# A gated scan whose two token halves run as two interleaved chains on shared split weights, with outputs laid out by token

## The chip, the core and the metric

The kernel runs on one core of a Trainium2 chip. That core has TensorE (PE in the profile; PEld is its weight load), VectorE (DVE), ScalarE (ACT), GpSimd (POOL) and SyncE (SP). Each engine executes its own instructions in the order in which they stand in its queue and waits for others by semaphores. The metric is the time of one launch on the device in microseconds (us).

## What is computed

A two-layer encoder on 1024 tokens of width 1024, in fp32. Layer 0 is windowed attention with a feed-forward block; layer 1 replaces attention by a bidirectional gated linear scan (HGRN2) of 8 heads of 128 keys and 128 values. The change touches only that scan. Cut to what matters:

```python
def step(state, inp):                       # one chunk of tokens, one direction
    qc, kc, vc, gc = inp
    b = jnp.cumsum(gc, axis=2)
    inter = jnp.einsum('bhtk,bhkv->bhtv', qc * jnp.exp(b), state)
    ...
    scores = jnp.einsum('bhtk,bhsk,bhtsk->bhts', qc, kc, decay)
    intra = jnp.einsum('bhts,bhsv->bhtv', scores, vc)
    ...
    return new_state, inter + intra
...
z = h @ w_in                                # q, f forward, f backward, v, gate
logf_f, k_f = forget(z[..., o1:o2], lb_fwd) # f = lb + (1-lb)*sigmoid, k = (1-lb)*(1-sigmoid)
...
o = out_f + out_b
o = o * lax.rsqrt(jnp.mean(o * o, axis=-1, keepdims=True) + LN_EPS) * norm_g
o = o * jax.nn.silu(gate)
return o.reshape(B, S, HGRN_VW) @ w_o
```

## The kernel before, in words

Every large product is made of three fp32r matmuls: operands are split into a high part (a ScalarE cast, line 73) and a low part (a subtraction on VectorE or GpSimd, line 74), and `mm3` (lines 349 to 351) multiplies high by high, high by low and low by high. Tokens come in two halves `h` of 512. Activations stand with features on partitions and tokens along the free axis; a pool `acts` of 49 buffers of 128x512 (function `A`) holds most of them, 32 of which are the split input X of the layer.

In the scan stage (`hgrn`), head `n` and half `h` go through these steps:

- `proj`: three projections `z(i, n, h)` of 24 matmuls each into a PSUM tile `zps`; ScalarE's sigmoid `sg`; VectorE makes the decay F and the key K for both directions from it (lines 1044, 1045), then the query and its two decayed forms Q (lines 1048, 1052). `v_proj` makes the values of two heads at once (`hvps`).
- `levels`: the scores of each block of 128 tokens are built in seven levels of doubling block size. In a level ScalarE copies K to `ks` (line 1074), VectorE multiplies K by the decay `cur` (line 1079), TensorE makes four 128x128 products `lv` (line 1082; two matmul instructions each in the profile), and VectorE multiplies both halves of Q (lines 1087, 1089), makes the decay of the next size `tot` (line 1093) and copies `lv` under a mask into the scores `sc` (line 1095). Q of a level waits for `lv` of that level, `lv` of the next level waits for Q and `ks`. Level 0 and the diagonal use sums over partitions by a matmul with ones (`average`, lines 395, 396).
- `states`: transposes of K (`tr`, `kt`), the products `u` with the values, and the running states S, a sequence of small VectorE operations over the four blocks.
- `out`: the output `op` with values on partitions (line 1162), then the root mean square over partitions by squares, a sum with ones (`ms`), a root on ScalarE, VectorE's reciprocal (line 1170) and a product (line 1172).
- `gate`: the fourth projection and two VectorE operations (lines 1036, 1037) which leave the gated output in `O`, in SBUF until the output projection (`hops`).

`weave(main, side, ratio)` runs two generators, one step of `main` and `ratio` steps of `side` at a time. Here `main` is the projections of the next half and a gate, `side` is `work`: levels, states and out of the present half. So before the change one chain of levels is under way at a time, and every projection weight is loaded and split twice, once per half (GpSimd makes the low part of `w_hz` and `w_hv`). `plan_all` lists the weights in the order in which they are taken. A scheduler then sets the final order on each engine from what is written, and a buffer that is taken again waits for its last reader.

## Time and profile before

| | us |
|---|---|
| median of three runs (2856.09 to 2858.42) | 2856.47 |
| the profiled execution | 2853.95 |
| its span in the trace | 2852.1 |
| attention, layer 0's feed-forward and its gate, up to | 1247 |
| gated scan, 1247 to 1955 | 708 |
| output projection of the scan, 1955 to 2050 | 95 |
| layer 1's feed-forward and gate, 2050 to 2852 | 802 |

TensorE is busy 95% of the span, VectorE 71%, GpSimd 48%, ScalarE 45%; the mean granted clock of TensorE is 0.985. In the rows below, "zps<-xh_n,w_hz" reads: writes tile zps, from tiles xh_n and w_hz; "[0.58 <-PE lv L1082]" is idle time before an instruction and what ended it. A line of a group has its count (x512), busy us, mean ns of one, and after the second bar the idle time before the group's instructions.

### The profile page before, as it was taken

How to read it: one execution, taken by the hardware profiler on the slowest of the kernel's cores; microseconds unless marked ns; L12 is line 12 of the kernel's file. 1: busy time of each engine (PE TensorE's matmuls, PEld its weight loads, DVE VectorE, ACT ScalarE, POOL GpSimd, SP SyncE). 2: the span in 40 equal slices, each digit the busy share in tenths (PEclk: the TensorE clock that was granted, in tenths of full speed). 3: DMA queues.
4: the chain of work that ended last, by engine and by line, in shares of the span. 5: the costliest groups of instructions: out<-in, count | busy, mean ns of one | idle time of the engine just before them, and what ended most of it. 6: DMA issues, size and time to landing. Idle time of an engine off the chain costs nothing.

```text
span 2852.1 us, 37180 instructions
## 1 busy us (share of the span) xinstructions
PE 2699.7 (95%) x12820; PEld 2173.5 (76%) x12820; DVE 2014.7 (71%) x2933; ACT 1283.2 (45%) x2334; POOL 1367.1 (48%) x958
## 2 busy tenths in 40 slices
PE   8999998999999999999998999989989999999999
PEld 6666676788887787787787877878767888878777
DVE  6778887755554658848888888898886555556685
ACT  4555667233333445534444443444462333344463
POOL 4243232656555747653443433331436556556563
PEclk9999999999999999999999999999999999999999
DMA  4111135444445953221111211112355444478243
GB/s 163 49 42 46 43 120 203 164 165 166 148 159 193 363 160 107 89 63 60 56 64 45 74 55 57 63 51 76 103 189 195 156 159 141 154 270 304 81 159 115
DMA packets 194877, 361.40 MB, mean 127 GB/s; under 512 B 22144, under 2 KB 24960, under 8 KB 194688
## 3 DMA queue, kind: packets, MB, share of 16 engines
q1 hardware_dynamic: 150624, 278.78, 29.4%
q10 hardware_dynamic: 44064, 80.24, 7.8%
q8 instruction: 101, 1.65, 0.2%
q14 instruction: 88, 0.72, 0.1%
HBM read 274.52 MB, written 84.41 MB: 126 GB/s over the span
## 4 chain that ended last, share of the span: by engine, by line
PE 36%; DVE 12%; issue 4%; POOL 3%; ACT 2%; DMA 1%; SPq 0%; ACTq 0%; POOLq 0%; DVEq 0%
PE x L349 3%; PE x L351 3%; PE x L350 3%; PE zps L351 2%; PE zps L349 2%; PE zps L350 2%; PE lv L1082 2%; POOL wo L74 2%; PE op L1162 1%; DVE K L1079 1%; PE zy L349 1%; PE zy L351 1%; PE zy L350 1%; DVE Q L1052 1%; PE pgps L350 1%
## 5 line engine op out<-in xcount | busy, mean ns | idle before, releaser
L74 POOL TENSOR_TENSOR w_hz<-r_hz,w_hz 128x512 fp32r<-128x512 f32 x128 | 180.6, 1418 | 332.4 <-ACT w_hz L73 323.0
L74 DVE TENSOR_TENSOR wp<-wraw,wp 128x512 fp32r<-128x512 f32 x200 | 210.7, 1054 | 163.2 <-ACT wp L73 135.8
L74 DVE TENSOR_TENSOR hs<-wraw,hs 128x512 fp32r<-128x512 f32 x154 | 210.9, 1388 | 139.7 <-ACT hs L73 136.4
L74 POOL TENSOR_TENSOR wo<-wraw,wo 128x512 fp32r<-128x512 f32 x154 | 225.7, 1478 | 158.1 <-ACT wo L73 143.5
L73 ACT CAST wp<-wraw 128x512 fp32r<-128x512 f32 x200 | 124.5, 623 | 295.5 <-PE x L351 149.0
L349 PE MATMUL x<-xc,wp 128*128 128x512 f32 x528 | 211.5, 402 | 12.6 <-ACT u L734 9.5
L349 PE MATMUL zps<-xh_n,w_hz 128*128 128x512 f32 x512 | 212.7, 415 | 0.0
L351 PE MATMUL x<-xc,wp 128*128 128x512 f32 x528 | 210.9, 400 | 0.0
L350 PE MATMUL x<-xc,wp 128*128 128x512 f32 x528 | 210.2, 398 | 0.0
L351 PE MATMUL zps<-xh_n,w_hz 128*128 128x512 f32 x512 | 202.4, 395 | 0.0
L350 PE MATMUL zps<-xl_n,w_hz 128*128 128x512 f32 x512 | 201.3, 393 | 0.0
L73 ACT CAST wo<-wraw 128x512 fp32r<-128x512 f32 x154 | 95.4, 620 | 188.7 <-POOL wo L74 114.4
L349 PE MATMUL ox<-hs,wo 128*128 128x512 f32 x352 | 138.4, 397 | 12.6 <-ACT hs L73 12.6
L186 POOL TENSOR_TENSOR wraw<-s,wraw 128x512 f32<-128x512 f32 x34 | 45.0, 1325 | 203.7 <-DVE wp L74 203.7
L351 PE MATMUL ox<-hs,wo 128*128 128x512 f32 x352 | 138.6, 394 | 1.6 <-POOL wo L74 1.6
L350 PE MATMUL ox<-hs,wo 128*128 128x512 f32 x352 | 138.8, 394 | 0.7 <-DVE hs L74 0.7
L349 PEld LDWEIGHTS x<-xc,wp 128*128 128x128 f32 x528 | 100.1, 190 | 40.0 <-ACT u L734 10.3
L1082 PEld LDWEIGHTS lv<-Q,ks 128*128 128x128 f32 x768 | 97.8, 191 | 37.3 <-issue 25.1
L1074 ACT COPY ks<-K 128x512 f32<-128x512 f32 x96 | 60.6, 631 | 145.4 <-DVE K L1079 111.3
L1082 PE MATMUL lv<-Q,ks 128*128 128x128 f32 x768 | 105.4, 279 | 20.4 <-DVE tot L1093 10.3
L73 ACT CAST w_hz<-r_hz 128x512 fp32r<-128x512 f32 x128 | 79.0, 618 | 89.8 <-issue 42.4
L351 PEld LDWEIGHTS x<-xc,wp 128*128 128x128 f32 x528 | 100.0, 189 | 25.3 <-DVE wp L74 0.6
(376 smaller groups left out, 8420.2 us busy)
## 6 DMA issues: line engine op xcount, KB each, us to landing
wraw<-in_wfi_dram SPq DMA_DIRECT2D x196, 256.0 KB, 3.1
wraw<-in_wfo_dram SPq DMA_DIRECT2D x154, 256.0 KB, 4.1
wraw<-h SPq DMA_DIRECT2D x154, 256.0 KB, 4.8
r_hz<-in_whg_dram SPq DMA_DIRECT2D x128, 256.0 KB, 2.8
wraw<-w SPq DMA_DIRECT2D x88, 256.0 KB, 5.3
w<-wraw ACTq DMA_DIRECT2D x66, 256.0 KB, 3.1
h<-th ACTq DMA_DIRECT2D x66, 256.0 KB, 2.1
r_pg<-in_wpg_dram SPq DMA_DIRECT2D x32, 512.0 KB, 3.8
```

The costliest lines, as they stand in the source:

```text
L73: act.copy(hi, src)
L74: (eng or dve).tensor_tensor(lo, src, f32(hi), op=ALU.subtract)
L186: pool.tensor_tensor(a11, tmp, a11, op=ALU.subtract)
L349: pe.matmul(ps, lhsT=w[0], rhs=x[0], start=start, stop=False, skip_group_check=free)
L350: pe.matmul(ps, lhsT=w[0], rhs=x[1], start=False, stop=False, skip_group_check=free)
L351: pe.matmul(ps, lhsT=w[1], rhs=x[0], start=False, stop=stop, skip_group_check=free)
L1052: dve.tensor_tensor(Qq[:, 1 - d], qk[:, 0], Fg[:, d], op=ALU.mult)
L1074: act.copy(view(ks, 0, [[2 * B, g], [B, 2], [1, B]]), kv)
L1079: dve.tensor_tensor(kv, kv, view(cur, off + 1, [[2, g], [row - 1, 2], [0, B]]), op=ALU.mult)
L1082: pe.matmul(lv[:, c], lhsT=ks[:, c * P:(c + 1) * P], rhs=view(Qq, c * P, dims), start=True, stop=True)
L1162: pe.matmul(op[:, cs], lhsT=a, rhs=b, start=i == 0, stop=i == len(ops) - 1)
```

## The change

Both halves of a head now run together. `proj` takes each weight once and multiplies it with both halves; `work(n)` advances the levels of half 0 and half 1 in turn (`both`, which takes one step of each of two generators), then states and out of both. Head 0 alone runs its halves one after the other. F and K are made on ScalarE by activations with scale and bias. The output is computed transposed, with tokens on partitions (`sc` and Q are now the stationary side): the sum of squares comes from ScalarE's accumulating Square in four blocks, the root from a GpSimd power and three small VectorE operations with one refining step, and the scaling from four ScalarE activations. `gated` transposes the output back on TensorE (`otr`), multiplies it by the gate, and stores it to DRAM (heads 0 to 6) until `split_o` reads it back. Gates come two heads later, within the next `proj`. Values, ks and states move from their own tags to the common pool of 49; F, K, qk, tot and Q get more buffers.

```diff
                 for i in (1, 2, 0):
                     z(i, n)
+                    if i == 1 and n > 1:
+                        z(3, n - 2)
 
             ffn(0)
             load(0)
             for n in range(NH):
                 load(n)
-                if n > 1:
-                    z(3, n - 2)
-                if n + 1 < NH:
-                    load(n + 1)
-                if n > 0:
-                    z(3, n - 1)
-                if n + 1 == NH:
-                    z(3, n - 1)
-            z(3, NH - 1)
-            z(3, NH - 1)
+            for n in (NH - 2, NH - 1):
+                z(3, n)
...
+                mh = gp.tile([P, 4], F32, bufs=1, name="mh")
+                dve.memset(mh, -0.5)
+                kept = {(n, h): D_(f"o{n}{h}") for n in range(NH) for h in range(2)}
...
+                    for h in hs:
+                        vt = [A(f"v{n}{h}").rearrange("p (b v) -> p b v", b=4) for n in (2 * pr, 2 * pr + 1)]
+                        V[2 * pr, h], V[2 * pr + 1, h] = vt
...
+                            for i in range(2):
+                                act.copy(vt[i][:, b], o[:, i * P:(i + 1) * P])
...
+                def z(i, n, hs):
+                    w = take_w("z", i, n)
+                    for h in hs:
+                        ps = yield from lin(w, [X[k][h] for k in range(KT)], "zps")
+                        sg = T("t0", "sg")
+                        act.activation(sg, ps, AF.Sigmoid)
+                        yield h, ps, sg
...
+                def gate(n, late=None):
+                    for r in z(3, n, (0, 1)):
+                        if r:
+                            h, ps, sg = r
+                            gz = A(f"gz{n}{h}") if late is not None else sg
+                            dve.scalar_tensor_tensor(gz, ps, ng[:, 0:1], sg, ALU.mult, ALU.mult)
+                            if late is not None:
+                                late[h] = gz
+                            else:
+                                gated(n, h, gz)
                         yield
...
-                    ps, sg = yield from z(3, n, h)
-                    dve.tensor_tensor(sg, sg, ps, op=ALU.mult)
-                    dve.scalar_tensor_tensor(O[n][h], O[n][h], ng[:, 0:1], sg, ALU.mult, ALU.mult)
-                    Fg, Kk = G("F", f"F{n}{h}", 2), G("K", f"K{n}{h}", 2)
+                def gated(n, h, gz):
+                    tr = aux("otr")
+                    for c in range(4):
+                        pe.transpose(tr[:, c * P:(c + 1) * P], O[n][h][:, c * P:(c + 1) * P], idn)
+                    o = A(f"og{n}{h}")
+                    dve.tensor_tensor(o, gz, tr, op=ALU.mult)
+                    if n < NH - 1:
+                        act.dma_start(kept[n, h], o)
+                    O[n][h] = o
...
+                def proj(n, hs):
+                    for h in hs:
+                        st[n, h] = dict(F=G("F", f"F{n}{h}", 3), K=G("K", f"K{n}{h}", 4))
                     for d in range(2):
-                        _, sg = yield from z(1 + d, n, h)
-                        dve.tensor_scalar(Fg[:, d], sg, om[:, d, n:n + 1], lb[:, d, n:n + 1], ALU.mult, ALU.add)
-                        dve.tensor_scalar(Kk[:, d], sg, 1.0, lbm[:, d, n:n + 1], ALU.subtract, ALU.mult)
-                    ps, sg = yield from z(0, n, h)
-                    qk = G("qk", f"qk{n}{h}", 1)
-                    dve.tensor_tensor(qk[:, 0], sg, ps, op=ALU.mult)
-                    pool.tensor_tensor(qk[:, 1], Kk[:, 0], Kk[:, 1], op=ALU.add)
-                    Qq = G("Q", f"Q{n}{h}", 3)
-                    for d in range(2):
-                        dve.tensor_tensor(Qq[:, 1 - d], qk[:, 0], Fg[:, d], op=ALU.mult)
-                    st[n, h] = dict(F=Fg, K=Kk, qk=qk, Q=Qq)
+                        for r in z(1 + d, n, hs):
+                            if r:
+                                t, sg = st[n, r[0]], r[2]
+                                act.activation(t["F"][:, d], sg, AF.Identity, bias=lb[:, d, n:n + 1], scale=om[:, d, n:n + 1])
+                                act.activation(t["K"][:, d], sg, AF.Identity, bias=om[:, d, n:n + 1], scale=lbm[:, d, n:n + 1])
+                            yield
+                        if d == 0 and n > 1:
+                            yield from gate(n - 2)
+                    for r in z(0, n, hs):
+                        if r:
+                            h, ps, sg = r
+                            t = st[n, h]
+                            qk = t["qk"] = G("qk", f"qk{n}{h}", 2)
+                            dve.tensor_tensor(qk[:, 0], sg, ps, op=ALU.mult)
+                            pool.tensor_tensor(qk[:, 1], t["K"][:, 0], t["K"][:, 1], op=ALU.add)
+                            Qq = t["Q"] = G("Q", f"Q{n}{h}", 4)
+                            for d in range(2):
+                                dve.tensor_tensor(Qq[:, 1 - d], qk[:, 0], t["F"][:, d], op=ALU.mult)
+                        yield
...
-                    tot = G("tot", f"tot{n}{h}", 1)
+                    tot = G("tot", f"tot{n}{h}", 2)
...
-                        ks = G("ks", "ks", 2, (HALF,))
+                        ks = A("ks")
...
-                    Ss = t["S"] = G("S", f"S{n}{h}", 2, (2, 4, P))
+                    Ss = t["S"] = [A(f"S{n}{h}{d}").rearrange("p (c v) -> p c v", c=4) for d in range(2)]
...
-                        ops = [(vt[:, c, vs], t["sc"][:, c])]
-                        if prev is not None:
-                            ops.append((prev, t["Q"][:, 1, cs]))
+                        ops = [(t["sc"][:, c], V[n, h][:, c])]
+                        if c or h:
+                            ops.append((t["Q"][:, 1, cs], t["S"][0][:, c] if c else st[n, 0]["Snext"]))
                         if not (h == 1 and c == 3):
-                            ops.append((t["S"][:, 1, c], t["Q"][:, 0, cs]))
+                            ops.append((t["Q"][:, 0, cs], t["S"][1][:, c]))
...
+                    ms, r = (gp.tile([P, 4], F32, tag=x, bufs=2, name=x) for x in ("ms", "r"))
                     sq = T("t0", "osq")
-                    act.activation(sq, op, AF.Square)
-                    ms = aux("ms")
-                    average(ms, onev, sq)
-                    rs = T("t1", "ors")
-                    act.activation(rs, ms, AF.Sqrt, bias=eps[:, 0:1], scale=1.0 / P)
-                    dve.reciprocal(rs, rs)
+                    for c in range(4):
+                        act.activation(sq[:, c * P:(c + 1) * P], op[:, c * P:(c + 1) * P], AF.Square, accum_out=ms[:, c:c + 1])
+                    dve.tensor_scalar(ms, ms, 1.0 / P, EPS, ALU.mult, ALU.add)
+                    pool.tensor_tensor(r, ms, mh, op=ALU.pow)
+                    dve.tensor_tensor(ms, ms, r, op=ALU.mult)
+                    dve.scalar_tensor_tensor(ms, ms, -0.5, r, ALU.mult, ALU.mult)
+                    dve.scalar_tensor_tensor(ms, ms, 1.5, r, ALU.add, ALU.mult)
+                    yield
                     O[n][h] = A(f"o{n}{h}")
...
-                    dve.tensor_tensor(O[n][h], rs, op, op=ALU.mult)
+                    for c in range(4):
+                        act.activation(O[n][h][:, c * P:(c + 1) * P], op[:, c * P:(c + 1) * P], AF.Identity,
+                                       scale=ms[:, c:c + 1])
...
+                def work(n):
+                    if n == 0:
+                        yield from levels(0, 0)
+                        while "Q" not in st.get((0, 1), ()):
+                            yield
+                        yield from levels(0, 1)
+                    else:
+                        yield from both(levels(n, 0), levels(n, 1))
+                    yield from states(n, 0)
+                    yield from states(n, 1)
+                    yield from both(out(n, 0), out(n, 1))
+
+                gzs = [None, None]
+                weave(load(0, (0,)), pend, 0.75)
                 for n in range(NH):
-                    def main0():
-                        yield from load(n, 1)
-                        if n > 1:
-                            yield from gate(n - 2, 0)
-
-                    def main1():
-                        if n + 1 < NH:
-                            yield from load(n + 1, 0)
-                        if n > 0:
-                            yield from gate(n - 1, 1)
-                        if n + 1 == NH:
-                            yield from gate(n - 1, 0)
-
-                    weave(main0(), work(n, 0), 0.75 if n % 2 else 0.5)
-                    weave(main1(), work(n, 1), 0.5 if n % 2 else 0.75)
+                    if n + 1 < NH:
+                        main = load(n + 1, (0, 1))
+                        if n == 0:
+                            main = chain(load(0, (1,)), main)
+                        count = (40 if n else 53) + (16 if n % 2 else 0)
+                        weave(main, work(n), (20 if n else 27) / count)
                 oh = [[], []]
...
-                    split(hi, lo, O[n][h])
+                    o = O[n][h]
+                    if n < NH - 1:
+                        o = A(f"or{n}{h}")
+                        sync.dma_start(o, kept[n, h])
+                    split(hi, lo, o)
...
-                weave(chain(gate(NH - 1, 0), gate(NH - 1, 1)), chain(out(NH - 1, 0), splits(0, 0, NH - 1), out(NH - 1, 1)), 2)
+                weave(chain(gate(NH - 2), gate(NH - 1, gzs), splits(0, 0, NH - 1)), work(NH - 1), 0.7)
+                for h in range(2):
+                    gated(NH - 1, h, gzs[h])
```

VectorE, the levels of head 4. Before, one chain: level 2 and the start of level 3 of half 0 (names end in head and half: K40 is K of head 4, half 0).

```order
L1079 TENSOR_TENSOR K40_13907<-K40_13907,tot40_14301 128x64x2x4
L1087 TENSOR_TENSOR Q40_14110<-Q40_14110,tot40_14301 128x128x2
L1089 TENSOR_TENSOR Q40_14110<-Q40_14110,tot40_14301 128x128x2
L1095 COPY_PREDICATED sc40_14291<-hm_10950,lv2_14343 128x512
L1093 TENSOR_TENSOR tot40_14301<-tot40_14301 128x2x64
L1079 TENSOR_TENSOR K40_13907<-K40_13907,tot40_14301 128x32x2x8
L1093 TENSOR_TENSOR tot40_14301<-tot40_14301 128x2x32
L1087 TENSOR_TENSOR Q40_14110<-Q40_14110,tot40_14301 128x64x4
```

Now, one round over both chains (K40, then K41):

```order
L1106 TENSOR_TENSOR K40_13938<-K40_13938,tot40_14448 128x64x2x4
L1114 TENSOR_TENSOR Q40_14341<-Q40_14341,tot40_14448 128x64x4
L1116 TENSOR_TENSOR Q40_14341<-Q40_14341,tot40_14448 128x64x4
L1120 TENSOR_TENSOR tot40_14448<-tot40_14448 128x2x64
L1122 COPY_PREDICATED sc40_14438<-hm_10950,lv3_14537 128x512
L1106 TENSOR_TENSOR K41_13940<-K41_13940,tot41_14474 128x64x2x4
L1114 TENSOR_TENSOR Q41_14408<-Q41_14408,tot41_14474 128x64x4
L1116 TENSOR_TENSOR Q41_14408<-Q41_14408,tot41_14474 128x64x4
L1120 TENSOR_TENSOR tot41_14474<-tot41_14474 128x2x64
L1122 COPY_PREDICATED sc41_14464<-hm_10950,lv3_14549 128x512
```

One chain's block of five operations has become two blocks, half 0's and half 1's, with nothing else between them in this head.

VectorE, from the end of a head's outputs to the next head's first level. Before, the two outputs of head 3 inside the first levels of head 4:

```order
L74 TENSOR_TENSOR avl_14150<-osq_14146,avh_14149 128x512
L1170 RECIPROCAL ors_14155<-ors_14155 128x512
L1036 TENSOR_TENSOR sg_14172<-sg_14172,zps_14133 128x512
L1172 TENSOR_TENSOR o31_14158<-ors_14155,op_14093 128x512
L1037 SCALAR_TENSOR_TENSOR o21_13389<-o21_13389,ng_10957,sg_14172 128x512
L74 TENSOR_TENSOR avl_14255<-osq_14251,avh_14254 128x512
L74 TENSOR_TENSOR avl_14295<-qk40_14107,avh_14294 128x512
L1170 RECIPROCAL ors_14260<-ors_14260 128x512
L74 TENSOR_TENSOR avl_14308<-ks_14303,avh_14307 128x512
L1172 TENSOR_TENSOR o30_14263<-ors_14260,op_14213 128x512
```

Now, the outputs of head 3 in front of the first level of head 4:

```order
L1079 TENSOR_TENSOR Q40_14341<-qk40_14338,F40_13937 128x512 x2
L1187 TENSOR_SCALAR ms_14344<-ms_14344 128x4
L1187 TENSOR_SCALAR ms_14356<-ms_14356 128x4
L1189 TENSOR_TENSOR ms_14344<-ms_14344,r_14345 128x4
L1189 TENSOR_TENSOR ms_14356<-ms_14356,r_14357 128x4
L1190 SCALAR_TENSOR_TENSOR ms_14344<-ms_14344,r_14345 128x4
L1190 SCALAR_TENSOR_TENSOR ms_14356<-ms_14356,r_14357 128x4
L1191 SCALAR_TENSOR_TENSOR ms_14344<-ms_14344,r_14345 128x4
L1191 SCALAR_TENSOR_TENSOR ms_14356<-ms_14356,r_14357 128x4
L1104 TENSOR_TENSOR ks_14450<-Q40_14341,K40_13938 128x256 x2
L1114 TENSOR_TENSOR Q40_14341<-Q40_14341,F40_13937 128x256
```

The two reciprocals, the low parts of the squares and the products with the root are gone; eight operations on 128x4 stand in their place, ahead of ks and Q of the next head, and `r` in them comes from GpSimd.

TensorE between two level groups of head 4. Before, from lv3 to lv4 of half 0:

```order
L350 MATMUL zps_14367<-xl_n41_11098,w_hz_12_4_14183 128x512
L351 MATMUL zps_14367<-xh_n41_11097,w_hz_12_4_14183 128x512
L349 MATMUL zps_14367<-xh_n51_11114,w_hz_12_4_14183 128x512
L350 MATMUL zps_14367<-xl_n51_11115,w_hz_12_4_14183 128x512
L351 MATMUL zps_14367<-xh_n51_11114,w_hz_12_4_14183 128x512
L349 MATMUL zps_14367<-xh_n61_11143,w_hz_12_4_14183 128x512
L350 MATMUL zps_14367<-xl_n61_11144,w_hz_12_4_14183 128x512
L351 MATMUL zps_14367<-xh_n61_11143,w_hz_12_4_14183 128x512
L349 MATMUL zps_14367<-xh_n71_11153,w_hz_12_4_14183 128x512
L350 MATMUL zps_14367<-xl_n71_11154,w_hz_12_4_14183 128x512
L351 MATMUL zps_14367<-xh_n71_11153,w_hz_12_4_14183 128x512
L1082 MATMUL lv4_14404<-Q40_14110,ks_14405 128x128 x4
```

Now, from lv4 of half 0 to lv4 of half 1:

```order
L343 MATMUL zps_14530<-xh_n61_11166,w_hz_13_4_14284 128x512
L1109 MATMUL lv4_14573<-Q40_14341,ks_14574 128x128 x4
L344 MATMUL zps_14530<-xl_n61_11167,w_hz_13_4_14284 128x512
L345 MATMUL zps_14530<-xh_n61_11166,w_hz_13_4_14284 128x512
L343 MATMUL zps_14530<-xh_n71_11176,w_hz_13_4_14284 128x512
L344 MATMUL zps_14530<-xl_n71_11177,w_hz_13_4_14284 128x512
L345 MATMUL zps_14530<-xh_n71_11176,w_hz_13_4_14284 128x512
L1109 MATMUL lv4_14585<-Q41_14408,ks_14586 128x128 x4
```

Twelve projection matmuls stood between two level groups; now five stand between the groups of the two halves.

## Rows read from the trace of the kernel before

**Rows 1.** Gated-scan stage: its length, busy time and instructions per engine, granted clock, DMA.

```profile
1247.00:1955.00 708.00, 651.93 (x3809) 557.84 (x3808) 602.12 (x936) 302.00 (x510) 262.94 (x185) 0.99 0.18 60
```

**Rows 2.** Costliest TensorE groups of 1247 to 1965: count, busy us, mean ns, idle before.

```profile
L349 PE MATMUL zps<-xh_n,w_hz 128*128 128x512 f32 x512 | 212.7, 415 | 0.0
L1019 PE MATMUL hvps<-w_hv,xh_n 128*128 128x256 f32 x225 | 64.7, 288 | 0.0
L1082 PE MATMUL lv<-Q,ks 128*128 128x128 f32 x768 | 105.4, 279 | 20.4 <-DVE tot L1093 10.3 <-DVE Q L1089 9.9
L1162 PE MATMUL op<-Q,S 128*128 128x128 f32 x208 | 38.0, 300 | 13.6 <-DVE S L1139 13.6
L1115 PE MATMUL u<-v,kt 128*128 128x128 f32 x256 | 37.1, 291 | 13.4 <-ACT kt L1111 13.4
```

**Rows 3.** TensorE's timeline: start, duration (a row of several: together), instruction.

```profile
1641.33 0.39 PE L351 MATMUL zps<-xh_n,w_hz 128*128 128x512 f32 x1
1641.56 0.60 PE L1109 MATMUL tr<-idn,K 128*128 128x128 f32 x4
1641.91 0.47 PE L349 MATMUL zps<-xh_n,w_hz 128*128 128x512 f32 x1
...
1658.90 1.12 PE L1082 MATMUL lv<-Q,ks 128*128 128x128 f32 x8
1659.77 0.49 PE L349 MATMUL zps<-xh_n,w_hz 128*128 128x512 f32 x1
...
1735.13 0.28 PE L1019 MATMUL hvps<-w_hv,xh_n 128*128 128x256 f32 x1
1735.25 0.28 PE L1020 MATMUL hvps<-w_hv,xl_n 128*128 128x256 f32 x1
```

**Rows 4.** Who TensorE waited for in 1247 to 1965: total us, times, longest.

```profile
PE op L1162 <- DVE S L1139: 13.6, 7, 2.7
PE u L1115 <- ACT kt L1111: 13.4, 6, 2.7
PE lv L1082 <- DVE tot L1093: 10.3, 5, 2.5
PE lv L1082 <- DVE Q L1089: 9.9, 13, 1.4
```

**Rows 5.** VectorE groups of 1247 to 1955, each shape apart: count, busy, mean.

```profile
L1095 DVE COPY_PREDICATED sc<-hm,lv 128x512 f32<-128x512 uint8 x112 | 81.6, 728 | 6.3 <-ACT sc L1062 5.0 <-PE lv L396 0.9
L1079 DVE TENSOR_TENSOR K<-K,tot 128x512 f32<-128x512 f32 x96 | 74.2, 773 | 2.8 <-ACT ks L1074 1.8
L1087 DVE TENSOR_TENSOR Q<-Q,tot 128x256 f32<-128x256 f32 x96 | 73.3, 763 | 15.2 <-PE lv L1082 14.1
L1089 DVE TENSOR_TENSOR Q<-Q,tot 128x256 f32<-128x256 f32 x96 | 62.8, 654 | 0.0
L1170 DVE RECIPROCAL ors<-ors 128x512 f32<-128x512 f32 x14 | 46.9, 3351 | 11.6 <-ACT ors L1169 11.6
L1044 DVE TENSOR_SCALAR F<-sg,om,lb 128x512 f32<-128x512 f32 x32 | 22.3, 697 | 20.2 <-ACT sg L1031 20.0
L1093 DVE TENSOR_TENSOR tot<-tot 128x128 f32<-128x128 f32 x16 | 7.3, 454 | 0.2
```

**Rows 6.** Timeline: a VectorE product started inside a GpSimd subtraction, and two alone.

```profile
1598.43 0.41 DVE L1089 TENSOR_TENSOR Q<-Q,F 128x256 f32<-128x256 f32 x1
1598.76 0.68 DVE L1079 TENSOR_TENSOR K<-K,tot 128x512 f32<-128x512 f32 x1
...
1639.74 1.47 POOL L74 TENSOR_TENSOR w_hz<-r_hz,w_hz 128x512 fp32r<-128x512 f32 x1
1639.99 1.51 DVE L1089 TENSOR_TENSOR Q<-Q,tot 128x256 f32<-128x256 f32 x1
```

**Rows 7.** GpSimd's largest group of 1247 to 1955.

```profile
L74 POOL TENSOR_TENSOR w_hz<-r_hz,w_hz 128x512 fp32r<-128x512 f32 x127 | 178.9, 1416 | 332.4 <-ACT w_hz L73 323.0 <-PE lv L1082 6.6 <-issue 2.0
```

**Rows 8.** ScalarE, whole span: an activation with scale and bias per partition.

```profile
L459 ACT ACTIVATE y<-y,lnt 128x512 f32<-128x512 f32 x48 | 38.0, 813 | 15.2 <-DVE y L458 15.0
```

92 lines of the change are left out of this document (37 added, 55 removed).

## Prediction

> **What bounds the kernel now.** I read the table of stages first, then the costliest groups inside the gated-scan stage, then the timeline of that stage for the pace of single instructions, then who waited for whom. The diff touches only the gated scan, which is the stretch from 1247 to 1955 us; everything before and after it issues the same work. There TensorE shows 651.93 of 708 us busy and VectorE 602.12, while ScalarE has 302 and GpSimd 263 [rows 1]. So TensorE bounds the stage, and VectorE is close behind it at 85%.
>
> A busy TensorE is not one at its pace, so I price its work by start-to-start distance. A 128x512 matmul starts 0.23 us after the one before, a 128x256 one 0.12, a group of eight level matmuls occupies 0.87 until the next projection matmul, four transposes 0.35 [rows 3]. Counts [rows 2]: 3 x 512 projections x 0.23 = 353 us; 3 x 225 value projections x 0.12 = 81; 768 / 8 level groups x 0.87 = 84; 256 state matmuls at 0.87 / 8 = 28; 352 output matmuls (11 products in each of 16 halves, two instructions each; 208 of them are the row's form) at 0.11 = 38; 32 groups of transposes (two per head and half, `states`) x 0.35 = 11; 96 averaging matmuls (lv0, lv1 and ms, two each, in 16 halves) x 0.23 = 22. That is 617 us, so some 92 of the 708 are stalls, refills behind them and slow-clock stretches (granted clock 0.99). This 92 is all that the change can win.
>
> TensorE's named waits are for VectorE or for something that VectorE delayed: `op` for S 13.6 us, `u` for kt 13.4, `lv` for tot 10.3 and for Q 9.9 [rows 4]. The reader should see VectorE running late there, with a reciprocal of 3.35 us per half in its queue [rows 5].
>
> **The change part by part.** TensorE's work is unchanged in sum. Each projection matmul still loads its own weights, so sharing the split weights between halves removes none. The 32 `ms` matmuls go (32 x 0.23 = -7.4 us) and 64 transposes of outputs come (16 x 0.35 = +5.6) [rows 3]: zero within 2 us. The four transposes in rows 3 last 0.60 us together and hold the next projection back by 0.35, one alone being far longer than its share. The Trainium skill (TensorE: Matmul & The Clock Gate, Part 4: PE-mode transpose) gives about 275 ns for a transpose inside a kernel, a rule against this change: 64 of them would be an estimated 17.6 us and the sum 12 us later; the spacing in this trace speaks for 0.09 us each.
>
> VectorE loses, per half: the reciprocal 3.35 us, two F and two K operations (F 0.70 each with its waits, K near it), the product with the root, and the low part of the square: 16 x 3.35 = 54 us and, by F's row taken for both, 64 x 0.70 = 45 us at most are the bulk [rows 5]. It gains four operations on 128x4 per half, far smaller than any row of its group.
>
> GpSimd splits each z weight tile once instead of twice: 64 x 1.416 = 91 us of 263 go, and half of the v weight splits with them [rows 7, 1]. This matters for VectorE: a 128x256 product takes 0.41 us alone and 1.51 us when it starts inside a GpSimd subtraction [rows 6], and the mean of that form in the stage is 0.763 and 0.654 [rows 5].
>
> ScalarE loses half of the casts and all root activations with their table loads; it takes over F and K (64 activations with pointer scale and bias, at most 0.813 us each [rows 8], 52 us) and 128 small activations on 128x128, each below 0.813. At 302 of 708 us [rows 1] it can take that beside TensorE; without that cover each would delay a level's ks copy.
>
> **The price: rounds that VectorE bounds.** Two chains now go through the seven levels side by side, so in a round VectorE does two blocks K, Q, Q, tot, sc. By the mean rows a block is 0.773 + 0.763 + 0.654 + 0.454 + 0.728 = 3.37 us [rows 5]; an instruction ends about 0.07 after the next one starts (0.41 long, the next 0.33 behind [rows 6]), so 3.02, or 6.0 a round. Without GpSimd beside it K is 0.68 and Q 0.41 [rows 6]; with tot at 0.3 (estimate, its row less the same interference) a block is 2.53 - 0.35 = 2.2 and a round 4.4. With GpSimd's splits halved I take the middle, 5.2; the ends are 4.4 and 6.0.
>
> In heads 2, 4, 6 the other half of TensorE's queue is z projections, and the new order puts 52 of them between lv2 and lv7 of head 4, beside ten level groups: (52 x 0.23 + 10 x 0.87 + 0.35) / 5 rounds = 4.2 us a round. So TensorE waits 1.0 us in each of 6 rounds, 18 us in three heads. In heads 1, 3, 5 a round has 24 to 30 value matmuls and two level groups, 4.6 to 5.3 us: 0.3 a round, 5 us. Head 7 has only the two last gates beside it: 6 us in its rounds. After its last level the chain transposes, kt, u, S, op, squares, power, O, otr, gate product, split runs with little else in the queue, and hops needs its end; some 10 us (estimate: about 13 us of dependent steps, against 15 hops matmuls, 3.4 us). Before, this last chain was shorter on its queue: one half was already out.
>
> At the end of each other head the three small VectorE operations wait for the GpSimd power. That operation stands in no row; between nothing and 1.42 us, a full tile's subtraction [rows 7], which is the nearest row, and I take the upper end, two per head. Behind it in VectorE's queue stand ks and Q of the next head's first level, and lv0 and lv1 on TensorE wait for these. The new order has 36 to 48 matmuls between op and lv0 (9.7 to 10.9 us) as cover; squares of both halves, a split in front, two powers, small products, ks, its cast and its low part are about as long. I take 1.5 us in seven heads, 10 us. Head 0 keeps its single chains (8 us, its share of 92 being about 11), and slow-clock stretches some 7 (clock 0.99).
>
> Output stores and reloads (28 x 256 KB) replace 80 weight loads of that size, at a DMA share of 0.18 [rows 1]; their issues sit on ScalarE's and SyncE's queues behind products that are done well before; I take nothing, and a reload that is late would show as ScalarE waiting before the first hops.
>
> Sum of stalls after: 18 + 5 + 6 + 10 + 10 + 8 + 7 = 64 against 92, so -28 us. The profiled execution took 2853.95 us; 2826. The median of the runs, 2856.47, stands 2.5 above it, so the forecast for runs is 2828.
>
> **Rivals.**
> Slower: VectorE's rounds stay at 6.04 us because the remaining GpSimd work falls into the rounds. Then 24 rounds (heads 2, 4, 6, 7) lose 1.84 and 18 lose 1.14: 65 us instead of the 29 counted above, +36: 2864. It beats the old time from a round of about 5.9 us up. For it: VectorE was 85% busy with one chain; against it: some 110 us of GpSimd work are gone.
> Much faster: rounds at 4.4 us lose 0.2 in 24 rounds, 5 us, the ends of heads are covered and the tail costs 5: stalls 25, -67: 2790. For it: all of TensorE's named waits are on late VectorE work; against it: even heads have only 4.2 us of TensorE work in a round.
> No change: the power waits behind a 1.42 us split on GpSimd twice per head, and VectorE, blocked, starts the next head 3.5 us late in seven heads: +25 on the forecast, 2853. For it: nothing in VectorE's queue may pass the waiting operation; against it: the 10 us of cover.
>
> **How the numbers follow.** Forecast 0.48, much faster 0.24, no change 0.12, slower 0.16. What this measurement tells from no change is about 0.2%, 5.7 us. Faster: 0.48 + 0.24 and a little of the third, 0.74; same 0.10; slower 0.16. The range for eight in ten is 2795 to 2862; the forecast's own range, from the two ends of a round (4.4 and 6.0, half-way each), is 2812 to 2845.
>
> **What would show it.** In the new profile the gated-scan stage should be near 680 us, VectorE busy about 450 there, GpSimd about 150. The Q product should fall from 0.76 to near 0.6 us mean. Rounds of heads 2, 4, 6 should last about 5.2 us, with TensorE's `lv` waiting for Q; in heads 1, 3, 5 it should hardly wait. `u` waiting for kt and `op` for S should shrink from 13 us each to a few, save in head 7. If VectorE is over 540 busy, or rounds exceed 5.9 us, the forecast is wrong towards slower; if `lv0` waits come to over 20 us, the power chain is the reason.

## The result and the profile after

The changed kernel takes 2837.3 us (2829.9 to 2839.3) against 2857.4 (2856.1 to 2860.5) before, both run on the same chip: ratio 0.9927, 95% interval 0.9914 to 0.9939. It is faster by 20 us, 0.7%. The forecast was 2828, the range 2795 to 2862. Direction and range held; the working behind them held in part only.

The profiled execution lasted 2838.45 us (span 2836.7). The first row is the gated-scan stage of the changed kernel in the columns of [rows 1]. Then come two of its stretches: the start of a head and the level rounds behind it. The number after the five engines is the granted clock.

```profile
1247.00:1930.00 683.00, 646.86 (x3845) 562.92 (x3843) 431.89 (x876) 286.52 (x642) 183.96 (x137) 0.98 0.13 41
...
1639.00:1648.00 9.00, 6.91 (x19) 4.77 (x20) 8.47 (x12) 3.63 (x7) 3.27 (x2) 0.62 0.09 29
1649.00:1675.00 26.00, 25.91 (x159) 22.33 (x159) 25.70 (x61) 11.78 (x20) 2.92 (x2) 1.00 0.06 21
```

VectorE's busy time fell from 602 to 432 us and GpSimd's from 263 to 184. In the rounds TensorE is busy without a gap at full clock. In the start of the same head it stands idle for a quarter of the time, and the mean granted clock of those 9 us is 0.62. Who TensorE waited for in the stage (total, times, longest) answers to [rows 4]:

```profile
PE lv L389 <- ACT avh L73: 14.1, 8, 2.7
PE lv L390 <- DVE avl L74: 12.1, 9, 2.5
PE op L1181 <- DVE S L1166: 2.7, 3, 0.9
PE lv L1109 <- DVE Q L1116: 2.0, 4, 0.7
PE u L1140 <- ACT kt L1136: 1.6, 3, 0.7
```

The four waits of before, 47 us, came down to 8 (6 here and 1.5 for an S of another line). The waits at L389 and L390, the two averages that open a head (lv0 and lv1), grew to 26 us; before, at the same two places, they were 6:

```profile
PE lv L395 <- ACT avh L73: 3.3, 4, 1.0
PE lv L396 <- DVE avl L74: 2.6, 4, 1.0
```

VectorE's, GpSimd's and ScalarE's groups in the changed kernel answer to [rows 5, 7, 8]; L1188 is the power that stood in no row before:

```profile
L1106 DVE TENSOR_TENSOR K<-K,tot 128x512 f32<-128x512 f32 x96 | 69.5, 732 | 1.7 <-ACT ks L1101 1.6
L1079 DVE TENSOR_TENSOR Q<-qk,F 128x512 f32<-128x512 f32 x32 | 44.7, 1434 | 0.3
L1114 DVE TENSOR_TENSOR Q<-Q,tot 128x256 f32<-128x256 f32 x96 | 44.6, 465 | 17.1 <-PE lv L1109 16.7
L1116 DVE TENSOR_TENSOR Q<-Q,tot 128x256 f32<-128x256 f32 x96 | 43.4, 452 | 0.0
```

```profile
L74 POOL TENSOR_TENSOR w_hz<-r_hz,w_hz 128x512 fp32r<-128x512 f32 x69 | 94.4, 1374 | 301.1 <-ACT w_hz L73 292.9 <-DVE S L1160 5.7 <-PE u L1140 2.5
L1188 POOL TENSOR_TENSOR r<-ms,mh 128x4 f32<-128x4 f32 x14 | 14.1, 1016 | 20.3 <-DVE ms L1187 20.3
```

```profile
L1065 ACT ACTIVATE F<-sg,lb,om 128x512 f32<-128x512 f32 x32 | 26.2, 819 | 0.3
```

The two Q products of a level fell from 0.763 and 0.654 us to 0.465 and 0.452, near the 0.41 that one takes alone [rows 6]. The new order of a start is in the timeline (start, duration, instruction):

```profile
1632.96 1.01 POOL L1188 TENSOR_TENSOR r<-ms,mh 128x4 f32<-128x4 f32 x1
1633.02 0.16 DVE L1189 TENSOR_TENSOR ms<-ms,r 128x4 f32<-128x4 f32 x1 [1.06 <-POOL r L1188]
1633.94 1.29 POOL L74 TENSOR_TENSOR w_hz<-r_hz,w_hz 128x512 fp32r<-128x512 f32 x1
1634.01 1.25 DVE L1189 TENSOR_TENSOR ms<-ms,r 128x4 f32<-128x4 f32 x1 [0.82 <-POOL r L1188]
...
1635.57 0.75 DVE L1104 TENSOR_TENSOR ks<-Q,K 128x256 f32<-128x256 f32 x2
1635.62 2.18 ACT L1195 ACTIVATE o<-op,ms 128x128 f32<-128x128 f32 x8 [4.16 <-DVE ms L1191]
1638.11 0.68 ACT L73 CAST avh<-qk 128x512 fp32r<-128x512 f32 x1
1638.84 0.50 PE L389 MATMUL lv<-avh,onev 128*128 128x512 f32 x1 [2.65 <-ACT avh L73]
1639.15 1.59 POOL L1087 TENSOR_TENSOR qk<-qk 128x512 f32<-128x512 f32 x1 [3.91 <-DVE qk L1075]
1639.52 3.44 DVE L1079 TENSOR_TENSOR Q<-qk,F 128x512 f32<-128x512 f32 x2
1642.89 0.68 DVE L74 TENSOR_TENSOR avl<-ks,avh 128x512 fp32r<-128x512 f32 x1
1643.62 0.79 PE L390 MATMUL lv<-avl,onev 128*128 128x512 f32 x1 [1.77 <-DVE avl L74]
```

ScalarE stood 4.16 us before the scalings of O, which wait for the power's chain, and the cast that TensorE needs stood behind them. Later two Q products took 3.44 us beside GpSimd's qk product and a split, and the low part for the next average stood behind these. The 128x4 product that lasts 0.16 us at 1633.02, inside a power, took 1.25 at 1634.01, ending 0.03 us after the subtraction it had started inside.

To say where time went, I took every pair of TensorE instructions that follow each other from the first value projection to the last output projection, and counted by how much their start distance exceeds the usual one of such a pair (its tenth percentile over the kernels compared). The usual distances sum to 706 us before and 706 after, so TensorE's work is unchanged by this count. The excess by part of a head (starts: from a head's first average to its level rounds; rounds: the level groups; states: transposes and the products u; outputs: op and what stands behind it; tail: behind the last head's outputs):

| Kernel | Median, us | Ratio to before | Stretch | Starts | Rounds | States | Outputs | Tail | At the lower clock |
|---|---|---|---|---|---|---|---|---|---|
| before | 2857.4 | | 812.1 | 9.6 | 38.3 | 25.3 | 29.4 | 2.3 | 20.5 |
| changed | 2837.3 | 0.9927 | 790.4 | 41.5 | 17.1 | 8.2 | 5.1 | 6.3 | 27.3 |
| e1 scalings later | 2838.2 | 0.9926 | 790.2 | 30.6 | 22.8 | 13.2 | 6.0 | 5.8 | 30.7 |
| e2 qk on VectorE | 2819.4 | 0.9867 | 774.5 | 28.7 | 15.8 | 7.8 | 5.2 | 5.3 | 10.2 |
| e3 no power | 2815.1 | 0.9850 | 775.3 | 30.5 | 16.0 | 8.2 | 6.1 | 4.2 | 13.7 |
| e4 splits twice | 2880.2 | 1.0080 | 831.1 | 57.6 | 33.4 | 7.9 | 9.4 | 5.7 | 54.6 |
| e5 one chain | 2877.8 | 1.0069 | 830.7 | 62.1 | 40.5 | 7.6 | 6.7 | 5.0 | 58.0 |
| e6 VectorE load back | 2829.3 | 0.9902 | 781.1 | 26.3 | 21.1 | 8.2 | 10.6 | 3.7 | 10.2 |
| e7 before, splits halved | 2836.0 | 0.9920 | 785.0 | 7.1 | 31.2 | 19.7 | 18.6 | 2.7 | 3.4 |
| e8 before, no reciprocal | 2858.0 | 1.0004 | 811.7 | 8.2 | 40.1 | 26.3 | 29.2 | 2.7 | 20.5 |
| e9 F, K on VectorE | 2838.7 | 0.9938 | 795.5 | 40.7 | 18.7 | 8.0 | 9.7 | 7.4 | 30.7 |
| e10 one power, qk | 2817.9 | 0.9868 | 775.4 | 28.8 | 18.3 | 7.9 | 5.2 | 5.3 | 10.2 |
| e11 the same, F, K | 2825.8 | 0.9896 | 777.3 | 29.2 | 17.4 | 8.2 | 7.9 | 4.9 | 17.1 |
| e12 e1 and e2 | 2815.5 | 0.9853 | 769.4 | 16.2 | 24.4 | 7.6 | 5.3 | 5.3 | 0 |

Times are in us. Some excess has no column (1 us before, 6 in the changed kernel). Stretch and excess are of the profiled execution, the medians of all runs. The profiled execution was the longest of its runs in e3 (8 us over the median), e9 and e12 (5 us), and the shortest in e7 (9 us under), so their rows may be off by about as much. One execution of e1 and one of before on its chip were far slower (4361 and 4079 us) and are in no ratio. Ratios are to the runs of before on the same chip, and half the width of their intervals is 0.0008 to 0.0015. "At the lower clock" is time at 1.2 instead of 2.4 GHz, already inside the excess: there a 128x512 matmul starts 0.42 us after the one before instead of 0.23, so 27.3 us of it cost some 12. All of the changed kernel's lie in starts of heads. So the change won 62 us in rounds, states and outputs (93.0 to 30.4) and gave back 36 in starts and tail and 5 in what has no column; 22 are left in the stretch. In this one execution the first value projection began 7.4 us later than before (1242.5 against 1235.1), with the mean clock ahead of it at 0.97 against 0.98, in code that the change doesn't touch; hence the profiled gain of 15.5 us and the runs' gain of 20.

### The profile page after: what moved, and what is told of

Read it like the earlier page. It is cut to its first block, busy times and chain, and to the rows that moved or that the text cites. A ratio compares the mean times of both kernels' runs of the same rounds, so it can differ in the third digit from the quotient of the medians.

```text
span 2836.7 us, 36978 instructions
## 1 busy us (share of the span) xinstructions
PE 2702.2 (95%) x12852; PEld 2182.9 (77%) x12852; DVE 1840.3 (65%) x2886; ACT 1267.7 (45%) x2482; POOL 1278.8 (45%) x904
## 3 DMA queue, kind: packets, MB, share of 16 engines
q8 instruction: 101, 1.65, 0.2%
## 4 chain that ended last, share of the span: by engine, by line
PE 38%; DVE 7%; POOL 4%; issue 4%; ACT 2%; DMA 1%; SPq 0%; ACTq 0%; POOLq 0%; DVEq 0%
PE zps L345 3%; PE zps L343 3%; PE zps L344 3%; PE lv L1109 3%; PE x L343 3%; PE x L345 3%; PE x L344 3%; POOL wo L74 2%; PE zy L343 1%; PE zy L345 1%; PE zy L344 1%; DVE Q L1079 1%; PE pgps L344 1%; PE pgps L345 1%; PE pgps L343 1%
## 5 line engine op out<-in xcount | busy, mean ns | idle before, releaser
L74 POOL TENSOR_TENSOR w_hz<-r_hz,w_hz 128x512 fp32r<-128x512 f32 x70 | 96.1, 1379 | 301.1 <-ACT w_hz L73 292.9
L343 PEld LDWEIGHTS x<-xc,wp 128*128 128x128 f32 x528 | 100.0, 189 | 37.4 <-ACT u L728 8.1
L345 PEld LDWEIGHTS x<-xc,wp 128*128 128x128 f32 x528 | 100.0, 189 | 25.4 <-DVE wp L74 0.6
L344 PEld LDWEIGHTS x<-xc,wp 128*128 128x128 f32 x528 | 100.0, 189 | 23.5
L345 PEld LDWEIGHTS zps<-xh_n,w_hz 128*128 128x128 f32 x512 | 97.4, 190 | 21.4 <-POOL w_hz L74 1.3
L344 PEld LDWEIGHTS zps<-xl_n,w_hz 128*128 128x128 f32 x512 | 97.7, 191 | 16.7
L343 PEld LDWEIGHTS zps<-xh_n,w_hz 128*128 128x128 f32 x512 | 97.5, 190 | 16.3
```

What stands on the lines that cost most here:

```text
L74: (eng or dve).tensor_tensor(lo, src, f32(hi), op=ALU.subtract)
L343: pe.matmul(ps, lhsT=w[0], rhs=x[0], start=start, stop=False, skip_group_check=free)
L344: pe.matmul(ps, lhsT=w[0], rhs=x[1], start=False, stop=False, skip_group_check=free)
L345: pe.matmul(ps, lhsT=w[1], rhs=x[0], start=False, stop=stop, skip_group_check=free)
```

## The experiments

**e1: the chain behind the power, moved.**

```diff
-    yield from both(levels(n, 0), levels(n, 1))
+    lv = both(levels(n, 0), levels(n, 1))
+    next(lv)
+    with tc.issue_after(mark[0].ins), tc.issue_after(mark[1].ins):
+        drain(rest.pop())
+    yield
+    yield from lv
...
```

(`rest` holds the part of `out` behind the power, `mark` the two instructions of the last split for an average.)

> The changed kernel, with the three small VectorE products behind the GpSimd power and the eight ScalarE scalings of O queued behind the first level's averages of the next head (the instructions stay the same). In the trace of the changed kernel 41.5 of 84.3 us by which TensorE's instruction starts exceed their usual spacing lie at the starts of heads (lv0, lv1). Theory A, the queues: VectorE's ks and ScalarE's casts stand behind the power's chain, so with the chain moved back the starts of heads 2, 4, 6 give some 5 us each and those of 1, 3, 5, 7 some 2 each: about 23 us, near 2815 (2808 to 2828), and the two average waits (14.1 us for avh, 12.1 for avl) fall below 10 together. Theory B, the neighbours: the starts are late because GpSimd's product and weight splits prolong VectorE's Q (1.43 us instead of about 0.7); then little moves, 2832 to 2840. Theory C: the last projection of the head ends too late for any order; no change, 2837.

Measured: 2838.2 us, 0.9926 (0.9913 to 0.9940): no gain over the changed kernel. The waits were:

```profile
PE lv L390 <- DVE avl L74: 11.9, 9, 2.8
PE lv L1110 <- DVE sc L1123: 5.6, 9, 0.8
PE lv L389 <- ACT avh L73: 4.3, 4, 1.6
```

and behind the start, on its timeline:

```profile
1644.04 2.14 ACT L1196 ACTIVATE o<-op,ms 128x128 f32<-128x128 f32 x8
1646.03 1.32 ACT L1102 COPY ks<-K 128x512 f32<-128x512 f32 x2
1646.78 1.30 DVE L1107 TENSOR_TENSOR K<-K,tot 128x512 f32<-128x512 f32 x2 [3.32 <-ACT ks L1102]
```

Theory A named a real queue: the wait for avh fell from 14.1 to 4.3 us. But in this head the scalings now stand ahead of the ks copies, and VectorE waits 3.32 us for these; over the stage starts gave 11 us, rounds and states took 11. The wait for avl stayed, as theory B says. As a forecast of the time, A failed; 2838 lies where B and C had it, though one of the two waits moved.

The same timeline shows that a power does not hold VectorE up: while they ran (the row holds two), a product took the 0.41 us that it takes alone [rows 6].

```profile
1628.35 2.79 POOL L1189 TENSOR_TENSOR r<-ms,mh 128x4 f32<-128x4 f32 x2 [0.71 <-DVE ms L1188]
1628.93 0.41 DVE L1115 TENSOR_TENSOR Q<-Q,F 128x256 f32<-128x256 f32 x1
```

**e2: GpSimd's product at the start, on VectorE.**

```diff
-    (dve if n == 0 else pool).tensor_tensor(qk[:, 1], qk[:, 0], qk[:, 1], op=ALU.mult)
+    dve.tensor_tensor(qk[:, 1], qk[:, 0], qk[:, 1], op=ALU.mult)
```

> The changed kernel, with the product of qk on VectorE in all heads instead of GpSimd in seven of them (14 instructions). Theory B (neighbours): the two Q products at each start fall from 1.43 to about 0.75 us each, avl of ks comes 1 to 2 us earlier in each of seven heads, 8 to 15 us in all: 2822 to 2830. Theory A (queues): the power chain still holds ks and the casts, so under 5 us: 2832 to 2838. Rival: VectorE's own 0.69 us stands in its queue in place of GpSimd's 1.66 and gives the time back: 2837 or a little over.

Measured: 2819.4, 0.9867 (0.9854 to 0.9880), 18 us below the changed kernel, more than theory B's 8 to 15.

```profile
L1079 DVE TENSOR_TENSOR Q<-qk,F 128x512 f32<-128x512 f32 x32 | 29.6, 963 | 0.3
```

```profile
PE lv L389 <- ACT avh L73: 12.3, 8, 2.1
PE lv L390 <- DVE avl L74: 5.3, 9, 1.0
```

The Q products fell from 1.434 to 0.963 us and the wait for avl from 12.1 to 5.3; the wait for avh fell little, from 14.1 to 12.3. Giving VectorE 14 more operations left it as busy as in the changed kernel (433 us against 432 in the same window), since those beside it got shorter. Of the 16 us by which the stretch fell, some 8 are clock: 10.2 us at the lower level instead of 27.3.

**e3: no power.**

```diff
-    pool.tensor_tensor(r, ms, mh, op=ALU.pow)
+    dve.tensor_scalar(r, ms, 0.0, 1.0, ALU.mult, ALU.add)
```

> The changed kernel, with the GpSimd power replaced by a VectorE operation on the same 128x4 tile that gives ones: the root is left out, so the outputs are scaled wrongly. It takes away the step to GpSimd and back (1.02 us of the power and some 0.8 to 1.1 us of VectorE waiting behind each, 16 times). Theory A: starts of heads come 2 to 4 us earlier, since there are two powers per head one behind the other; 10 to 20 us in all, 2817 to 2827; less than moving the whole chain, since the eight scalings still stand ahead of the casts. Theory B: 2833 to 2838.

Measured: 2815.1, 0.9850 (0.9835 to 0.9865), 22 us below: theory A's 10 to 20 and a little over.

```profile
PE lv L390 <- DVE avl L74: 10.7, 9, 2.3
PE lv L389 <- ACT avh L73: 7.3, 8, 1.6
```

The wait for avh halved, that for avl moved little. As a forecast of the time theory A holds and B fails; but the wait for avl, for which e2 shows B's cause, is still there.

**e4: GpSimd's load back.**

```diff
     split(hl[:, 0, :n], hl[:, 1, :n], raw[:, :n], eng)
+    if name.startswith("hz"):
+        pool.tensor_tensor(hl[:, 1, :n], raw[:, :n], f32(hl[:, 0, :n]), op=ALU.subtract)
```

> The changed kernel, with GpSimd's subtraction for each z weight tile made twice into the same tile: GpSimd gets back the 64 subtractions of some 1.4 us that the change took away. Theory of the prediction (the slower rival): VectorE's rounds go back towards 6.0 us through GpSimd's interference, the mean of the Q products goes from 0.46 to over 0.65 us, and the rounds lose 1 us and more in heads 2, 4, 6: 2850 to 2865. Theory D: rounds are paced by TensorE with slack on VectorE, so longer Q products are hidden for the most part: 2838 to 2846.

Measured: 2880.2, 1.0080 (1.0068 to 1.0093): 43 us above the changed kernel and slower than before. Neither theory's place was right. The rounds of heads 2, 4, 6 lasted 4.6 us on average, not 6 (VectorE's last operation of one round to that of the next; 4.2 to 4.3 without the load), though the second and third of each head took 5.8 and 6.2; the Q products took 0.55 and 0.59 us. Rounds and starts each took 16 us more, and the lower clock doubled; some 12 of the 41 us in the stretch are its part. That the weights came later is no rival: TensorE waited for the doubled low parts once, 3.4 us.

**e5: one chain after the other.**

```diff
-    yield from both(levels(n, 0), levels(n, 1))
+    yield from chain(levels(n, 0), levels(n, 1))
```

(and the weave's ratios follow the longer chain: 27 steps for 20, and 0.95 for 0.7 beside the last head).

> The changed kernel with the two halves' levels one chain after the other instead of side by side; shared weights, outputs and everything else stay. Theory I, interleaving is what pays: with one chain a level's ks copy, K, Q and matmuls follow one another with nothing between, TensorE waits for Q and tot again as before the change, and the time goes back to 2850 and more. Theory G, GpSimd's halved splits are what pays (doubling them cost 43 us): one chain at a time does as well, since TensorE has projections to put between; 2830 to 2842, and the starts of heads, now one half at a time, may even be shorter.

Measured: 2877.8, 1.0069 (1.0057 to 1.0082): theory I.

```profile
PE lv L1109 <- DVE Q L1116: 14.3, 13, 2.1
```

TensorE waits for Q again, 14.3 us instead of 2.0. Interleaving is worth 40 us inside the new order: without it there are two starts per head (62.1 us) and the rounds lose 40.5. Before, with one chain too, starts lost 9.6 and rounds 38.3. So the new order makes a start dear, and with one chain there are twice as many; which part of the order does so was not taken apart here.

**e6 and e9: VectorE's load back, and its smaller part alone.**

```diff
+    rq = T("t1", "rq")
+    dve.reciprocal(rq, op)
...
-    act.activation(t["F"][:, d], sg, AF.Identity, bias=lb[:, d, n:n + 1], scale=om[:, d, n:n + 1])
-    act.activation(t["K"][:, d], sg, AF.Identity, bias=om[:, d, n:n + 1], scale=lbm[:, d, n:n + 1])
+    dve.tensor_scalar(t["F"][:, d], sg, om[:, d, n:n + 1], lb[:, d, n:n + 1], ALU.mult, ALU.add)
+    dve.tensor_scalar(t["K"][:, d], sg, 1.0, lbm[:, d, n:n + 1], ALU.subtract, ALU.mult)
```

(The reciprocal, in `out`, is in e6 alone.)

> The changed kernel with VectorE's old load put back: a reciprocal of op (128x512, its result not used) per half, and F and K made by VectorE instead of ScalarE. That is some 16 x 3.35 + 64 x 0.7 = 98 us of VectorE work in the stage. Theory V, VectorE's own load made the old stalls: much of the 20 us gain goes, 2850 to 2860. Theory G: VectorE has over 200 us idle in the stage and GpSimd's share is what counts; the reciprocals stand in the queue at starts of heads, though, 1 to 2 us a head: 2842 to 2850.

> The changed kernel with F and K made by VectorE as before, nothing else. It tells which part of the last pair made the time fall by 8 us. If F and K on ScalarE (64 operations of 0.81 us in the queue of the casts and sigmoids) are what holds up the starts of heads: 2820 to 2827, and less than with the reciprocals added (2829). If the fall came from a luckier placing of the power chain and the reciprocals: 2834 to 2840.

Measured: 2829.3 (0.9889 to 0.9915) and 2838.7 (0.9925 to 0.9952). In the changed order F and K make no difference on either engine. With the reciprocals VectorE has 507 us of work in the stage instead of 432, and the kernel is 8 us faster: both theories missed. In e6's timeline the head's first cast of avh stands at 1628.31, ahead of the scalings at 1633.68; in the changed kernel behind them. The edit moves nothing on ScalarE by itself, so the scheduler's order is another one, for this cast like the one that e1 set by hand (the next two, at 1637.68 and 1638.20, stay behind the scalings). That this order is the whole of the 8 us was not tested apart.

**e7: the kernel before with half of the splits.** For the second half's z weights the high part is used as the low part.

```diff
...
+    if name.startswith("hz2"):
+        act.copy(hl[:, 0, :n], raw[:, :n])
+        return v[:, 0], v[:, 0]
     split(hl[:, 0, :n], hl[:, 1, :n], raw[:, :n], eng)
...
```

(`hz2` names the second half's weights.)

> The kernel before, with GpSimd's low part made for the first half's z weights alone; for the second half the high part is taken in its place (its z values come out about twice as large, so the outputs differ). TensorE, ScalarE, the DMAs and VectorE issue the same as before; GpSimd loses 64 subtractions of 1.42 us. Theory G: this alone gives most of what the change gave or more: 2815 to 2840, with Q products near 0.55 us instead of 0.76 and 0.65. Theory V: without VectorE's relief the reciprocal still stands in the queue: 2848 to 2857.

Measured: 2836.0, 0.9920 (0.9908 to 0.9933): 21 us from this alone, as much as from the whole change. VectorE still does its reciprocals, and its waits shrank:

```profile
PE u L1119 <- ACT kt L1115: 11.0, 6, 2.3
PE lv L1086 <- DVE tot L1097: 8.8, 4, 2.5
PE op L1166 <- DVE S L1143: 8.2, 7, 1.5
PE lv L1086 <- DVE Q L1093: 5.8, 5, 1.4
```

```profile
L1091 DVE TENSOR_TENSOR Q<-Q,tot 128x256 f32<-128x256 f32 x96 | 61.8, 644 | 30.4 <-PE lv L1086 29.3
L1093 DVE TENSOR_TENSOR Q<-Q,tot 128x256 f32<-128x256 f32 x96 | 53.1, 553 | 0.0
```

The Q products fell from 0.763 and 0.654 us to 0.644 and 0.553, one of them to theory G's 0.55. Over the whole stretch the same 1046 VectorE operations took 636 us instead of 683: this is GpSimd's interference, taken away by itself. Earlier weights are no rival, since TensorE had no wait for GpSimd's low parts in the stage before. Of the 27 us by which the stretch fell, some 8 are clock (3.4 us at the lower level against 20.5). Its profiled execution was the shortest of its runs (2827.4), so its 785.0 flatters it.

**e8: the kernel before without the reciprocal.**

```diff
-    dve.reciprocal(rs, rs)
+    dve.tensor_scalar(rs, rs, 0.5, 0.0, ALU.mult, ALU.add)
```

> The kernel before, with the reciprocal of the root replaced by a VectorE product with a constant on the same tile (the outputs are scaled wrongly): 3.35 us becomes 0.4 to 0.7 us, 16 times. Theory V: op waits for S (13.6 us), u for kt (13.4) and lv for tot and Q (20 together) come from late VectorE work, so 16 x 1 to 1.5 us: 2833 to 2841. Theory G: VectorE's lateness comes from the operations that GpSimd prolongs; 2850 to 2857.

Measured: 2858.0, 1.0004 (0.9995 to 1.0012): nothing.

```profile
L1170 DVE TENSOR_SCALAR ors<-ors 128x512 f32<-128x512 f32 x14 | 6.0, 425 | 11.9 <-ACT ors L1169 11.9
```

```profile
PE lv L1082 <- DVE Q L1089: 16.8, 15, 2.4
PE u L1115 <- ACT kt L1111: 14.1, 7, 2.7
PE op L1162 <- DVE S L1139: 13.6, 7, 2.7
```

VectorE lost 41 of its 47 us of reciprocals, and the waits for S and kt stood where they were (13.6 and 14.1 us against 13.6 and 13.4); those for Q and tot came to 18.3 together, against 20.2. Theory V is dead for the reciprocal: the longest operation on a nearly full engine was worth nothing.

**e10 and e11: towards a better version.** One power per head with qk on VectorE; then F and K on VectorE too.

```diff
-    yield from both(out(n, 0), out(n, 1))
+    yield from out(n)
...
+    ms, r = (gp.tile([P, 8], F32, tag=x, bufs=2, name=x) for x in ("ms", "r"))
```

(`out(n)` takes both halves; their squares fill the 8 columns.)

> The changed kernel with one power for both halves of a head (a 128x8 tile instead of two of 128x4, so one step to GpSimd and back per head instead of two) and the qk product on VectorE. If the power's chain and GpSimd's neighbouring product are two separate causes of the late starts, as 2815 without the power and 2819 without the product suggest, their gains add in part: 2803 to 2814, and the two average waits of TensorE fall from 26 us to under 12. If both removed the same wait: 2815 to 2820.

> The kernel with one power per head and the qk product on VectorE, and F and K on VectorE as well. If ScalarE's queue is a third cause: 5 to 10 us below the former, 2796 to 2808. If VectorE now becomes the late one in the rounds (it gets 64 operations of 0.55 us back): the same as the former or up to 5 us slower.

Measured: 2817.9 (0.9854 to 0.9881) and 2825.8 (0.9882 to 0.9910). The first adds nothing to e2 and lies where the rival, that both removed the same wait, had put it. But it doesn't decide between the two: one power on twice the width takes 1.65 us against 2.03 for two single ones, so the chain hardly got shorter.

```profile
L1193 POOL TENSOR_TENSOR r<-ms,mh 128x8 f32<-128x8 f32 x8 | 13.2, 1648 | 120.8 <-DVE ms L1192 120.8
```

In e11 the outputs' excess rose from 5.2 to 7.9 us; why F and K cost 8 us here and nothing in e9 stays open.

**e12: e1 and e2 together.** Both diffs.

> The changed kernel with both single edits: the power's small products and the scalings of O queued behind the first averages of the next head, and the qk product on VectorE. Alone the first took away the wait for avh (14.1 to 4.3 us) but not the wait for avl (11.9), and gave the time back where the scalings stand ahead of the ks copies of the second level; alone the second took 18 us. If the two waits are separate, the starts of heads fall well under the 28.7 us of excess that the second edit leaves, and the scalings cost some 10 us in the rounds again: 2810 to 2820. If the scalings in the rounds weigh as much as the starts they free, as in the first run: 2818 to 2824.

Measured: 2815.5, 0.9853 (0.9839 to 0.9866), the fastest with the whole computation, if not separable from e2.

```profile
PE lv L1110 <- DVE sc L1123: 6.2, 9, 0.9
PE lv L389 <- ACT avh L73: 4.3, 4, 1.6
PE lv L390 <- DVE avl L74: 3.5, 3, 1.2
```

```profile
1241.00:2011.00 770.00, 742.52 (x4329) 638.32 (x4328) 507.54 (x1013) 338.87 (x743) 202.23 (x148) 1.00 0.16 54
```

The two waits at starts are 8 us instead of 26, no part of the stretch ran at the lower clock, and the scalings cost 7 us in the rounds again. Each edit alone left the other's wait (11.9 for avl in e1, 12.3 for avh in e2), together both waits are small: the two causes are separate. In time e1's edit is not shown to add anything to e2's.

## Why the prediction was right, and where it was not

- **TensorE's work unchanged within 2 us: right.** The usual distances sum to 706 us on both sides of the change by the count above. The rule of the Trainium skill (TensorE: Matmul & The Clock Gate, Part 4: PE-mode transpose) fits the duration of a single transpose (0.272 us in the new trace), not its cost in the queue: four of them, at 1594.94, took 0.44 us to the next instruction.
- **GpSimd's halved splits matter for VectorE: right, and more than that.** The prediction let them pick a round between 4.4 and 6.0 us. e7 shows that on the old order they give the whole 20 us alone, e4 that the new order with the load put back is slower than before.
- **VectorE's relief: wrong.** The reading of [rows 4, 5], "VectorE running late there, with a reciprocal of 3.35 us per half in its queue", took the longest operation for the cause. e8 takes it away and gains nothing; e6 puts one like it back, with F and K, and loses nothing. (The sum had no term for this relief, so the error cost the forecast nothing. F and K taken from VectorE in the old order were not tested.)
- **Rounds, 18 + 5 + 6 us: too large.** A round of heads 2, 4, 6 was to take 5.2 us on VectorE against 4.2 on TensorE. It took 4.3, 4.2 and 4.2: TensorE's pace was right, VectorE's wrong, since the Q products went to 0.46 us, not the middle of 0.41 and 0.76. Rounds exceed by 12.4 us outside head 0 (17.1 less 4.7; head 0 itself took 8.1 with its starts, for which 8 had been set aside).
- **Starts of heads, 10 us, and slow clock, 7: too small, and the step that failed most.** Starts exceed by 38 us outside head 0, clock included. The power's chain was named and is real (e3, 22 us); its duration, set at the upper end of 1.42, measured 1.02. Missed were the eight scalings that stand on ScalarE between the chain and the casts (e1, where the wait goes and the time stays), GpSimd's qk product, untouched by the change, beside Q (e2, 18 us), and that TensorE's clock falls at such pauses (27.3 us at the lower level, all in starts). By the prediction's test, "if `lv0` waits come to over 20 us, the power chain is the reason", the 26 us at L389 and L390 name the chain; but without the power (e3) 18 of them are still there, and without the neighbour (e2) 17.6.
- **Tail, 10 us: near.** Tail and last states exceed by 7.3 (6.3 and 1.0).
- **Sum.** Forecast -28 in stalls; -22 in the stretch. Rounds were some 17 us too dear, the tail 3; starts with their clock were 21 too cheap, and 12 us in states and outputs before the last head, with 6 that the table gives no column, had no term at all: 84 us of stalls where 64 were forecast, on a base of 106 where 92 was counted. Errors of both signs left the sum nearly right, so the agreement is in part luck.
- **The slower rival** (rounds at 6 us through GpSimd's remaining work) had a real mechanism: e4 shows it with the old load, at 43 us, but in starts and clock as much as in rounds. The rival "no change" had priced a power that waits behind a split; its place was right, and its 25 us on the forecast is near the 21 that starts took over their term, but its mechanism was not: GpSimd stood idle before the powers until VectorE's mean square came (20.3 us in all, L1188).
- **Signs.** VectorE at 432 us and the stage's length came out near the forecast's 450 and 680; GpSimd at 184 us was busier than its 150, and the Q products at 0.46 were shorter than its 0.6.

## What to carry to other kernels

When two engines slow each other, take away the neighbour's work first, by itself: half of GpSimd's subtractions of projection weights were worth as much here as a rewrite (e7, whose outputs differ), while the longest operation of the nearly full engine was worth nothing (e8). Price a change at the points where all chains begin or end together, engine queue by engine queue, and not by the mean load; and count a pause of TensorE with the time at the lower clock that may come with it. An added 50 us of VectorE work came with another order on ScalarE and a gain of 8 us (e6), so one order says little about an operation's price.

## What the runs showed of the hardware

- A VectorE operation on two tensors in SBUF that starts inside a GpSimd subtraction, sum or product waits for its end: 1.25 us for a 128x4 product of otherwise 0.16. In the scan stage of the changed kernel 49 started in this way with more of the GpSimd operation left than they take alone, and 46 ended with it (before the change 124 of 132). Operations with an input in PSUM kept their times, 23 of 23 (S 0.347 us on average, two in 0.73 at 1697.14, inside GpSimd's sum of K from 1697.03 to 1698.32). So did operations that started inside a power (the 128x4 product at 1633.02, the Q product of e1 at 1628.93). The Trainium skill (SBUF — State Buffer, SBUF: two separate sides) says that the two engines share one port pair, locked for a whole instruction when a VectorE operation with two inputs in SBUF meets a GpSimd operation that reads SBUF. The trace agrees for subtractions, sums and products; for the power it does not, and there the measurement decides.
- GpSimd's power takes 1.02 us on 128x4 and 1.65 on 128x8: about 0.16 per added column.
- In the changed kernel TensorE's granted clock in the stage fell only in starts of heads, at its waits; before, it fell at six of the waits for kt and S. With the waits at starts down to 8 us (e12) it was 1.00 throughout.
